# Hybrid four-mixer layer: the first attention pair is combined behind the third head's first branch, with one statistics buffer and shifted tiles

## The chip, the cores and the metric

The kernel runs on one core of a Trainium2 chip. The metric is the device time of one execution in microseconds (us). The core has TensorE (PE; its weight loads are listed as PEld), VectorE (DVE), ScalarE (ACT), GpSimd (POOL) and SyncE (SP), which here issues the transfers. Each runs its own queue of instructions in order and waits on semaphores. SBUF is the on-chip memory, PSUM holds the results of TensorE.

## The reference

One layer over 2048 tokens of width 1024: RMSNorm, one input projection to 13 slices of 256 columns, four mixers of which each is multiplied by the SiLU of a gate, one output projection, RMSNorm, residual. The change touches mixer A, a causal attention of four heads of 64. Each head is computed with three dilations (1, 4, 16) over blocks of 128, and the three results are weighted by their softmax denominators:

```python
for window, dil in DILATED_PAIRS:              # (128, 1), (512, 4), (2048, 16)
    o, lse = _dilated_branch(q, k, v, window, dil, slopes)
    outs.append(o); lses.append(lse)
w = jax.nn.softmax(jnp.stack(lses), axis=0)
o = jnp.einsum('gbhs,gbhsd->bhsd', w, jnp.stack(outs))
...
y = jnp.concatenate([ya * silu(ag), yb * silu(bg), yc * silu(cg), yd * silu(dg)], -1)
y = jnp.einsum('bse,ed->bsd', y, w_out)
return x + _rms_norm(y, post_g)
```

## The kernel before

All matrix products are made from fp32 values split in a high and a low part, with two or three matmuls for each product.

First stage (to about 690 us): in two halves of 1024 tokens the input is normalised and transposed (`hh`, `hl`), and projected. `proj_t` multiplies a weight tile of 128 columns (`w128`, three buffers) by 512 tokens into `ps_t`; `proj_m` has the tokens as weights and streams the 256 column tile (`w256`, one buffer, pool `pa`) into `ps_m`: 256 columns for each matmul. The mixers B, C and D are finished here. Queries, keys, values and the gate of mixer A go to DRAM (`qk_d`, `v_d`, `ag_d`), the finished parts to `yb_d`.

Attention stage (690 to about 925 us): `attention(p, tab)` does a pair of heads, p = 0 for the first and second, p = 1 for the third and fourth. For each head it loads `q2`, `k2a`, `k2b` and does the branches in the order dil 4, 16, 1. All these loads and the reordered `q2b` share seven buffers of 8 KiB (tag "m8"). `branch` computes scores (`ps_s`, L98), the exponentials (L652 on VectorE, L654 on ScalarE), transposes them (`ps_pt`, PSUM tag "t", three buffers), splits them (`pt_hi` L661, `pt_lo` L662), multiplies by the values (`ps_o`, two banks), and `finish` writes the result to `o01` or `o2` (L676, L677). For dil 4 and 16 `keep_stats` stores the statistics through DRAM (`std`, L742, L745); for dil 1 they are in `sv`, the others are read back (`sraw`, L603), and `weigh` (L751 to L768) makes the weights `wt`.

`combine` then takes a pair: three small transposes `ps_w` for each half of the tokens, sixteen products `ps_f` that spread the weights over a head's rows (also tag "t"), multiplications on VectorE (L789, L790), and for each 512 tokens two additions (L791, L792), the gate (`sga` loaded L796, multiplied L797) and the split into `ysa` (L809, L810; one buffer of 256 tokens), stored to `ya_d` (L811). For the first pair the elementwise part runs on GpSimd. `o2` and `wt` have one buffer each, `o01` is another tile in each pair.

Between them lie nine `partial(t)`: the output projection of 128 tokens over the mixers B, C and D (`ps_out`, stored to `part_d`, L849). They come last in the program, and `issue_after` holds each behind a chosen value product (`marks`).

In the last stage the second pair is combined and `final` finishes the tokens.

The order on each engine's queue is set when the program is built: a planner simulates the engines, and of the instructions it holds ready it takes the one that stands earlier in the program. On the chip the queues run in that fixed order. A tile that reuses a buffer waits until everything that used the earlier tile is done.

The names `align0` and `align1` are tiles that nothing uses; they shift those behind them.

Of the kernel before, what the change touches and what calls it, by code (L numbers as in the profile page):

```python
# [9 lines left out]
F32 = mybir.dt.float32  # L10
# [8 lines left out]
P = 128  # L19
SEQ = 2048  # L20
DM = 1024
KT = DM // P
GRP = 512
# [65 lines left out]
def hymba(ctx: ExitStack, tc: tile.TileContext, x, pre_g, w_in, sgu_g, sgu_w, sgu_b, pool_w,  # L89
          pool_scale, ret_g, w_out, post_g, cmix, catt, out, dbg=None, npart=9, spread=(0.3, 0.95)):  # L90
    nc = tc.nc
    V, A, G, T, D = nc.vector, nc.scalar, nc.gpsimd, nc.tensor, nc.sync
# [10 lines left out]
    cp = ctx.enter_context(tc.tile_pool(name="const", bufs=1))  # L103
# [15 lines left out]
    ya_d = [scratch(f"ya{g}", [P, 2, GRP]) for g in range(NG)]  # L119

    ident = cp.tile([P, P], F32, name="ident")
    cp.tile([P, 96], F32, name="align0")
    for _ in range(2):
        small.tile([P, 8], F32, tag="align1", name="align1")

# [22 lines left out]
    with ExitStack() as c1:  # L148
# [42 lines left out]
        W2 = 6  # L191
        hT = {}
        first = []

        def prologue(gs, step):

# [43 lines left out]
        def weights(col, n, eng=V, scales=(1.0,)):  # L240

            if n == P:
                w = p1.tile([P, 2, KT, n], F32R, tag="w128", bufs=3, name="w128")
            else:
                w = pa.tile([P, 2, KT, n], F32R, tag="w256", bufs=1, name="w256")
            kc = KT * P // n
            for k in range(0, KT, kc):
                raw = p1.tile([P, kc, n], F32, tag="raw", bufs=2, name="raw")
                D.dma_start(raw, w_src[:, k:k + kc, col:col + n])
                for i, sc in enumerate(scales):  # L250
                    cs = slice(i * n // len(scales), (i + 1) * n // len(scales))
                    hi, lo = w[:, 0, k:k + kc, cs], w[:, 1, k:k + kc, cs]
                    A.activation(hi, raw[:, :, cs], AF.Copy, scale=sc)  # L253
                    if sc == 1.0:
                        eng.tensor_tensor(lo, raw[:, :, cs], r32(hi), ALU.subtract)  # L255
                    else:
                        V.scalar_tensor_tensor(lo, raw[:, :, cs], sc, r32(hi), ALU.mult, ALU.subtract)
            return w
# [298 lines left out]

    marks = []

    def attention(p, tab):  # L560
        o01 = (big if p == 0 else po).tile([P, 2, SEQ], F32, tag="big" if p == 0 else "o01", name="att_o01")
        o2 = po.tile([P, SEQ], F32, tag="o2", name="att_o2")
        o = [o01[:, 0], o01[:, 1], o2]
        wt = pc.tile([P, 3, 2, 2, 2, 8], F32, tag="wt", bufs=1, name="wt")
        for s in range(2):
            h = 2 * p + s
            rows = slice(s * HD, (s + 1) * HD)
            other = slice((1 - s) * HD, (2 - s) * HD)
            q2 = pm.tile([P, SEQ], F32R, tag="m8", bufs=7, name="q2")
            k2a = pm.tile([P, SEQ], F32R, tag="m8", bufs=7, name="k2a")  # L570
            k2b = pm.tile([P, SEQ], F32R, tag="m8", bufs=7, name="k2b")
            D.dma_start(r32(q2[rows]), qk_d[0][p][rows, 0])
            D.dma_start(r32(q2[other]), qk_d[0][p][rows, 1])
            for z in (rows, other):
                D.dma_start(r32(k2a[z]), qk_d[1][p][rows, 0])
                D.dma_start(r32(k2b[z]), qk_d[1][p][rows, 1])
            for b, dil in enumerate(DILS):
                vt = pm.tile([P, 16, 2 * HD], F32R, tag="m8", bufs=7, name="att_v")
                dst = r32(vt)
                if dil == 1:  # L580
                    src = v_d[h].rearrange("(n t c) d -> c t n d", c=4, t=32)
                    for c in range(4):
                        D.dma_start(dst[c * 32:(c + 1) * 32], src[c])
                elif dil == 4:
                    D.dma_start(dst.rearrange("q (j c) d -> q j (c d)", j=4),
                                v_d[h].rearrange("(j q c) d -> q j (c d)", j=4, c=4))
                else:
                    D.dma_start(dst.rearrange("q r d -> q (r d)"), v_d[h].rearrange("(q r) d -> q (r d)", r=16))
                qb = q2
                if dil != 1:  # L590
                    qb = pm.tile([P, SEQ], F32R, tag="m8", bufs=7, name="q2b")
                    if dil == 4:
                        src = r32(q2).rearrange("p (j k c i) -> p c j k i", j=4, c=4, i=8)
                        dst = qb.rearrange("p (j c k i) -> p c j k i", j=4, c=4, i=8)
                        for c in range(4):
                            (V if c < 3 else G).tensor_copy(dst[:, c], src[:, c])
                    else:
                        V.tensor_copy(qb.rearrange("p (r w i) -> p r w i", r=16, i=8),
                                      r32(q2).rearrange("p (w r i) -> p r w i", r=16, i=8))
                if dil == 1:  # L600
                    sv = p2.tile([P, 3, 2, 16], F32, tag="sv", bufs=2, name="sv")
                    raw = p2.tile([64, P], F32, tag="sT", bufs=1, name="sraw")
                    D.dma_start(raw, st_d[h].rearrange("b z (n q) -> (b z n) q", q=P))  # L603
                    branch(h, dil, qb, k2a, k2b, vt, tab, o[b], sv[:, b])
                    weigh(sv, raw, wt[:, :, :, s])
                    continue
                st = p2.tile([P, 2, 16], F32, tag="stat", bufs=2, name="att_st")
                branch(h, dil, qb, k2a, k2b, vt, tab, o[b], st)
                keep_stats(h, b, dil, st)
        return o01, o2, wt  # L610

    def branch(h, dil, q2, k2a, k2b, vt, tab, o, st):
# [119 lines left out]
    def keep_stats(h, b, dil, st):  # L732

        pt = ps2.tile([P, GRP], F32, tag="t", bufs=N_T, name="ps_st")
        transpose(pt[:32, :P], st.rearrange("p z n -> p (z n)"))
        sT = p2.tile([32, P], F32, tag="sT", bufs=1, name="sT")
        V.tensor_copy(sT, pt[:32, :P])
        for z in range(2):
            dst, src = st_d[h][b, z], sT[z * 16:(z + 1) * 16]
            if dil == 4:  # L740
                for j in range(4):
                    D.dma_start(dst.rearrange("(j k c i) -> j c k i", j=4, k=16, c=4)[j],  # L742
                                src[j * 4:j * 4 + 4].rearrange("c (k i) -> c k i", i=8))
            else:
                D.dma_start(dst.rearrange("(w r i) -> r w i", r=16, i=8), src.rearrange("r (w i) -> r w i", i=8))  # L745
# [68 lines left out]
    def load_y(t, pool):  # L814
        raw = pool.tile([P, 6, P], F32, tag="yraw", bufs=2, name="yraw")
        D.dma_start(raw, yb_d[t // 4][:, t % 4])
        return raw

    def split_y(raw, pool, eng):

        ys = []
        for e in range(0, 6, 3):
            yt = pool.tile([P, 3, 2, P], F32R, tag="yt", bufs=2, name="yt")
            src = raw[:, e:e + 3]
            if eng is A:
                A.activation(yt[:, :, 0], src, AF.Copy)
            else:
                eng.tensor_copy(yt[:, :, 0], src)
            G.tensor_tensor(yt[:, :, 1], src, r32(yt[:, :, 0]), ALU.subtract)
            ys += [yt[:, j] for j in range(3)]  # L830
        return ys
# [12 lines left out]
    def partial(t):  # L844
        z = p3.tile([P, DM], F32, tag="z", bufs=2, name="z")
        ys = split_y(load_y(t, p3), p3, G)
        for n in range(2):
            A.activation(z[:, n * GRP:(n + 1) * GRP], out_proj(ys, range(2, 8), n, ps2, "part"), AF.Copy)
        D.dma_start(part_d[t * P:(t + 1) * P], z)  # L849
# [33 lines left out]
    with ExitStack() as c2:  # L883
        pm = c2.enter_context(tc.tile_pool(name="pm", bufs=1, reuse_waits="tile"))
        p2 = c2.enter_context(tc.tile_pool(name="p2", bufs=1, reuse_waits="tile"))
        ps2 = c2.enter_context(tc.tile_pool(name="ps2", bufs=2, space=PSUM, reuse_waits="tile"))
        tab = pm.tile([P, T_HEAD], F32, name="tab")
        D.dma_start(tab, catt)
        raw = p3.tile([P, DM], F32, tag="z", bufs=2, name="sel_raw")[:32]
        D.dma_start(raw, cmix[:32, C_SEL:])  # L890
        G.tensor_copy(sel, raw.rearrange("r (n m) -> r n m", m=P))
        o = attention(0, tab)
        for i in (1, 2, 3):
            out_weights(i, V if i == 2 else G)
        combine(0, o, ps2, "t", False, range(0, SEQ, GRP), G)
        o = attention(1, tab)
        for t in range(npart):
            with tc.issue_after(marks[int(len(marks) * (t + spread[0]) / npart * spread[1])]):
                partial(t)
        out_weights(0, G)  # L900
# [45 lines left out]
```

## Time and profile before

| what | value |
|---|---|
| median of 3 runs | 1059.02 us (1055.12 to 1059.49) |
| profiled execution | 1055.14 us, span 1053.4 us |
| granted TensorE clock, mean | 0.981 |
| ScalarE, VectorE, GpSimd busy | 376.4, 519.1, 228.0 us |
| DMA | 128.91 MB, mean 122 GB/s |

A row of the profile's groups gives line, engine, operation, the tiles read and written and the count, then busy time and the mean duration of one. A row of a timeline gives start and duration in us, and in brackets the idle time before it and what ended that. "L98" is the helper in which every matmul is recorded, "L101" that of the transposes.

### The profile page before, as it was taken

The numbers are of one execution on the slowest core, as the hardware profiler recorded it, in microseconds if no ns is written. First come the engines' busy times: TensorE is split into PE (matmuls) and PEld (weight loads), VectorE is DVE, ScalarE is ACT, GpSimd is POOL, SyncE is SP. The second block draws the span as 40 slices with busy tenths as digits, with TensorE's granted clock in tenths as the row PEclk, the third lists the DMA queues.
The fourth block names the chain that finished last, engine by engine and source line by source line (L and its number), as shares of the span: only waits on it lengthen the run. The fifth ranks groups of instructions, "written<-read, shape, count | busy, mean of one in ns | idle before, by whom it ended". The sixth has DMA issues, their size and how long they took to land.

```text
span 1053.4 us, 15825 instructions
## 1 busy us (share of the span) xinstructions
PE 1000.1 (95%) x5960; PEld 861.6 (82%) x5960; DVE 519.1 (49%) x1584; ACT 376.4 (36%) x871; POOL 228.0 (22%) x217
## 2 busy tenths in 40 slices
PE   5899999999999999999999999988999989899994
PEld 5889898998888998989898888777896979776773
DVE  7621215687323331031666222176876667727776
ACT  6320313132212431031221111297873878612231
POOL 2310002221133000002120124031116411313444
PEclk9999999999999999999999999996999989989998
DMA  7530222332423232040310661187474663445565
GB/s 284 146 100 21 81 80 81 121 107 72 123 68 103 91 95 65 1 140 34 128 61 21 154 179 41 62 219 203 102 212 141 161 202 77 154 142 181 175 250 220
DMA packets 110988, 128.91 MB, mean 122 GB/s; under 512 B 9888, under 2 KB 88992, under 8 KB 108864
## 3 DMA queue, kind: packets, MB, share of 16 engines
q1 hardware_dynamic: 110912, 127.90, 39.7%
q8 instruction: 47, 0.77, 0.3%
q14 instruction: 29, 0.24, 0.1%
HBM read 91.57 MB, written 36.31 MB: 121 GB/s over the span
## 4 chain that ended last, share of the span: by engine, by line
PE 82%; DMA 7%; DVE 6%; ACT 2%; issue 2%; POOL 1%; SPq 1%; DVEq 0%; POOLq 0%; ACTq 0%
PE ps_t L98 38%; PE ps_m L98 16%; PE ps_out L98 10%; PE ps_s L98 4%; PE ps_o L98 4%; PE ps_pt L101 3%; PE ps_of L98 2%; DMA out_dram<-z 2%; DMA k2b<-qk 2%; DMA cm<-in_cmix_dram 1%; PE ps_in L98 1%; POOL z L877 1%; PE ps_mix L98 1%; DMA raw<-in_w_in_dram 1%; PE ps_x L101 1%
## 5 line engine op out<-in xcount | busy, mean ns | idle before, releaser
L98 PE MATMUL ps_t<-hh,w 128*128 128x512 f32 x1152 | 366.9, 395 | 0.0
L98 PEld LDWEIGHTS ps_t<-hh,w 128*128 128x128 f32 x1152 | 215.9, 188 | 47.8 <-issue 3.4
L98 PE MATMUL ps_t<-hl,w 128*128 128x512 f32 x576 | 226.1, 393 | 0.0
L98 PE MATMUL ps_m<-w,hh 128*128 128x256 f32 x1024 | 190.1, 286 | 1.6 <-ACT hh L235 1.6
L98 PEld LDWEIGHTS ps_m<-w,hh 128*128 128x128 f32 x1024 | 161.3, 193 | 3.3 <-ACT hh L235 2.2
L98 PE MATMUL ps_out<-wo,yt 128*128 128x512 f32 x576 | 153.9, 406 | 0.6 <-DVE z L875 0.6
L98 PE MATMUL ps_m<-w,hl 128*128 128x256 f32 x512 | 147.7, 288 | 0.1
L98 PEld LDWEIGHTS ps_t<-hl,w 128*128 128x128 f32 x576 | 108.3, 188 | 23.2 <-issue 1.4
L98 PEld LDWEIGHTS ps_out<-wo,yt 128*128 128x128 f32 x576 | 105.6, 192 | 23.1 <-issue 2.8
L255 DVE TENSOR_TENSOR w<-raw,w 128x1024 fp32r<-128x1024 f32 x42 | 58.5, 1402 | 109.5 <-ACT w L253 109.5
L98 PEld LDWEIGHTS ps_m<-w,hl 128*128 128x128 f32 x512 | 98.8, 193 | 0.8 <-DVE hl L236 0.3
L253 ACT ACTIVATE w<-raw 128x1024 fp32r<-128x1024 f32 (+1 forms) x56 | 55.0, 997 | 67.7 <-PE ps_t L98 37.3
L652 DVE CUSTOM_DVE_ANT_0 att_p<-ps_s,tab 128x128 f32<-128x128 f32 (+1 forms) x192 | 60.6, 360 | 36.3 <-PE ps_s L98 29.6
L662 DVE TENSOR_TENSOR pt_lo<-ps_pt,pt_hi 128x512 fp32r<-128x512 f32 x80 | 51.5, 652 | 18.6 <-ACT pt_hi L661 18.2
L654 ACT ACTIVATE att_p<-att_p,att_st 128x128 f32<-128x128 f32 (+1 forms) x128 | 55.0, 433 | 6.9 <-DVE att_st L652 6.4
L98 PE MATMUL ps_o<-pt_hi,att_v 128*128 128x128 f32 (+1 forms) x204 | 53.9, 284 | 1.7 <-DVE att_o L677 1.7
L98 PE MATMUL ps_o<-pt_lo,att_v 128*128 128x128 f32 (+1 forms) x204 | 52.9, 294 | 0.4 <-DVE pt_lo L662 0.4
L101 PE MATMUL ps_pt<-ident,att_p 128*128 128x128 f32 x300 | 50.6, 285 | 2.7 <-ACT att_p L654 2.5
L449 POOL TENSOR_TENSOR d_g<-d_g,ret_b 128x512 f32<-128x512 f32 x8 | 10.4, 1296 | 184.6 <-ACT d_g L447 184.6
L661 ACT ACTIVATE pt_hi<-ps_pt 128x512 fp32r<-128x512 f32 x80 | 44.1, 565 | 12.0 <-PE ps_pt L101 6.4
L98 PEld LDWEIGHTS ps_o<-pt_hi,att_v 128*128 128x128 f32 x204 | 41.0, 201 | 4.3 <-DVE att_o L677 1.9
L877 POOL TENSOR_TENSOR z<-z,xr 128x1024 f32<-128x1024 f32 x15 | 35.8, 2390 | 32.4 <-DVE z L875 27.7
(174 smaller groups left out, 1409.9 us busy)
## 6 DMA issues: line engine op xcount, KB each, us to landing
raw<-in_w_in_dram SPq DMA_DIRECT2D x52, 512.0 KB
qk<-qk_s SPq DMA_DIRECT2D x16, 512.0 KB
att_v<-vd SPq DMA_DIRECT2D x8, 1024.0 KB
xr<-in_x_dram SPq DMA_DIRECT2D x16, 512.0 KB
out_dram<-z SPq DMA_DIRECT2D x15, 512.0 KB
xt<-in_x_dram SPq DMA_DIRECT2D x7, 1024.0 KB
yraw<-yb SPq DMA_DIRECT2D x16, 384.0 KB
partd<-z SPq DMA_DIRECT2D x9, 512.0 KB
```

The lines of the kernel that those rows point to most:

```text
L98: return T.matmul(o, lhsT, rhs, start=start, stop=stop, skip_group_check=True)
L101: T.transpose(o, i, ident[:n, :n])
L253: A.activation(hi, raw[:, :, cs], AF.Copy, scale=sc)
L255: eng.tensor_tensor(lo, raw[:, :, cs], r32(hi), ALU.subtract)
L449: G.tensor_tensor(o, o, ret_b.unsqueeze(1).broadcast_to([P, 2, 256]), ALU.mult)
L652: V.tensor_tensor_reduce(out=pr[:, u, :w], in0=ps[:, u, :w], in1=bb, scale=-SLOPES[h] * HD ** -0.5, scalar=3e38, op0=ALU.add, op1=ALU.min, ...
L654: A.activation(pr[:, u, :w], pr[:, u, :w], AF.Exp, bias=neg, scale=-1.0, accum_out=st[:, 1, n:n + 1])
L661: A.activation(hi, pt[:, :w], AF.Copy)
L662: V.tensor_tensor(lo, pt[:, :w], r32(hi), ALU.subtract)
L877: (V if last else G).tensor_tensor(z[:, ns], z[:, ns], xr[:, ns], ALU.add)
```

## The change

`combine` of the first pair no longer stands between the two calls of `attention`. It is passed as `between` to the second call and stands behind the third head's dil 4 branch and its `keep_stats`. For that `o2` and `wt` of a pair are asked for only at its first dil 1 branch. `sv`, which had two buffers in `p2`, is one tile of the constant pool, in the place of the 384 bytes of `align0`. In `pa` an unused tile of 448 bytes stands ahead of `w256` and one of 64 bytes behind it, and one of 480 bytes in `p3` behind the tiles of `partial`.

```diff
-    cp.tile([P, 96], F32, name="align0")
+    svs = cp.tile([P, 3, 2, 16], F32, name="sv")
...
+        align = []
...
             else:
+                if not align:
+                    align.append(pa.tile([P, 112], F32, name="align2"))
                 w = pa.tile([P, 2, KT, n], F32R, tag="w256", bufs=1, name="w256")
+                if len(align) == 1:
+                    align.append(pa.tile([P, 16], F32, name="align3"))
...
-    def attention(p, tab):
+    def attention(p, tab, between=None):
         o01 = (big if p == 0 else po).tile([P, 2, SEQ], F32, tag="big" if p == 0 else "o01", name="att_o01")
-        o2 = po.tile([P, SEQ], F32, tag="o2", name="att_o2")
-        o = [o01[:, 0], o01[:, 1], o2]
-        wt = pc.tile([P, 3, 2, 2, 2, 8], F32, tag="wt", bufs=1, name="wt")
+        o = [o01[:, 0], o01[:, 1]]
...
                 if dil == 1:
-                    sv = p2.tile([P, 3, 2, 16], F32, tag="sv", bufs=2, name="sv")
+                    if s == 0:
+                        o2 = po.tile([P, SEQ], F32, tag="o2", name="att_o2")
+                        o.append(o2)
+                        wt = pc.tile([P, 3, 2, 2, 2, 8], F32, tag="wt", bufs=1, name="wt")
+                    sv = svs
...
                 keep_stats(h, b, dil, st)
+                if between and s == 0 and b == 0:
+                    between()
...
         ys = split_y(load_y(t, p3), p3, G)
+        if t == 0:
+            p3.tile([P, 120], F32, name="align4")
...
-        combine(0, o, ps2, "t", False, range(0, SEQ, GRP), G)
-        o = attention(1, tab)
+        o = attention(1, tab, lambda o=o: combine(0, o, ps2, "t", False, range(0, SEQ, GRP), G))
```

## The prediction

> **What bounds the kernel now.** I read the page first (engine shares, the chain that ended last), then the busy time by stretch, then the waits and the timelines around the moved step.
>
> ```profile
> PE 1000.1 (95%) x5960; PEld 861.6 (82%) x5960; DVE 519.1 (49%) x1584; ACT 376.4 (36%) x871; POOL 228.0 (22%) x217
> PE 82%; DMA 7%; DVE 6%; ACT 2%; issue 2%; POOL 1%; SPq 1%; DVEq 0%; POOLq 0%; ACTq 0%
> 50.00:350.00 300.00, 299.84 (x1779) 257.57 (x1778) 119.28 (x320) 70.27 (x98) 51.93 (x59) 1.00 0.27 86
> 385.00:690.00 305.00, 303.11 (x1794) 260.08 (x1793) 100.80 (x282) 61.90 (x98) 46.34 (x47) 1.00 0.29 85
> 787.00:847.00 60.00, 58.46 (x359) 49.13 (x359) 40.01 (x153) 37.95 (x123) 28.97 (x35) 1.00 0.55 148
> 847.00:855.00 8.00, 3.56 (x26) 2.99 (x25) 4.13 (x10) 3.38 (x11) 2.75 (x4) 0.81 0.83 218
> 855.00:860.00 5.00, 5.00 (x23) 4.47 (x23) 3.72 (x12) 4.45 (x13) 1.06 (x2) 0.62 0.98 390
> 787.00:856.00 69.00, 63.02 (x387) 53.12 (x387) 44.15 (x164) 42.27 (x136) 32.16 (x39) 0.97 0.59 160
> 856.00:912.00 56.00, 56.00 (x384) 51.16 (x384) 42.11 (x151) 45.59 (x139) 7.84 (x11) 0.97 0.35 107
> 912.00:927.00 15.00, 10.85 (x46) 8.38 (x45) 8.42 (x16) 6.10 (x12) 6.21 (x5) 0.78 0.86 294
> ```
>
> The columns of a stretch are its length, then PE, PEld, DVE, ACT and POOL busy, the granted clock, the DMA share and GB/s. TensorE is full in the projections (299.84 of 300 us), so nothing can be gained there except by faster matmuls. In the attention stage the moved step's stretch, 787 to 847, is also full (58.46 of 60): the output projections of `partial` are there to fill TensorE when attention cannot go on. Behind it comes a hole, 847 to 855, in which 8.00 - 3.56 = 4.44 us are idle, followed by a stretch at a clock of 0.62. From 856 to 912 TensorE is full again, and at 912 there is a second hole.
>
> The waits of TensorE from 787 to 860 name what ended each idle time (total, times, longest):
>
> ```profile
> PE ps_s L98 <- DMA k2b<-qk: 4.1, 1, 4.1
> PE ps_w L101 <- DVE wt L768: 1.2, 1, 1.2
> PE ps_o L98 <- DVE att_o L677: 0.3, 1, 0.3
> PE ps_pt L101 <- DVE att_o L790: 0.3, 1, 0.3
> ```
>
> So the combine of the first pair costs TensorE directly only 1.2 us (its first transpose waits for the weights) and 0.3 us (an attention transpose waits for a PSUM buffer that the combine held). The large wait, 4.1 us, is the fourth head's first score waiting for its `k2b`.
>
> **What the moved step does now.** Its timeline on TensorE, the queue of SyncE, ScalarE and GpSimd:
>
> ```profile
> 794.24 0.38 PE L101 MATMUL ps_w<-ident,wt 128*32 128x128 f32 x2 [1.21 <-DVE wt L768]
> 798.14 0.79 PE L98 MATMUL ps_f<-wr,sel 32*128 32x384 f32 x3
> 801.44 4.47 PE L98 MATMUL ps_out<-wo,yt 128*128 128x512 f32 x18
> 811.22 0.97 PE L98 MATMUL ps_f<-wr,sel 32*128 32x384 f32 x3
> 812.46 1.05 PE L101 MATMUL ps_pt<-ident,att_p 128*128 128x128 f32 x7 [0.27 <-DVE att_o L790]
> 806.45 0.41 ACT L809 ACTIVATE ysa<-att_o 128x256 fp32r<-128x256 f32 x1
> 855.06 0.42 ACT L809 ACTIVATE ysa<-att_o 128x256 fp32r<-128x256 f32 x1 [4.63 <-DMA ya<-ysa]
> 855.56 0.73 POOL L810 TENSOR_TENSOR ysa<-att_o,ysa 128x256 fp32r<-128x256 f32 x1 [5.73 <-ACT ysa L809]
> 856.48 0.59 ACT L676 ACTIVATE att_o<-ps_o 64x512 f32<-64x512 f32 x1
> 841.28 0.56 SPq L811 DMA_DIRECT2D ya<-ysa  x1
> 841.94 1.08 SPq L745 DMA_DIRECT2D std<-sT  x2
> 846.58 0.46 SPq L603 DMA_DIRECT2D sraw<-std  x1
> 847.13 1.19 SPq L576 DMA_DIRECT2D k2b<-qk  x2
> 847.73 6.90 DMA k2b<-qk
> ACT ysa L809 <- DMA ya<-ysa: 12.5, 5, 4.6
> SPq L811 <- POOL ysa L810: 15.3, 6, 5.9
> ya<-ysa SPq DMA_DIRECT2D x8, 256.0 KB
> ```
>
> Three things are to be seen. First, from 798 to 812 the sixteen `ps_f` products pass before any attention transpose: both use PSUM tag "t" with three buffers, and the combine stands ahead in the program. Second, the combine has a long tail: eight `ysa` copies through one buffer, each waiting for the store of the one before, from 806.45 to 855.06. The pair's `o2` has one buffer too, so the third head's dil 1 branch cannot write its first result before the last `ysa` is read: that result is the L676 at 856.48, right behind the L810 at 855.56. Third, SyncE's queue runs in order: it held a `ya` store (waiting for GpSimd, up to 5.9 us), then statistics, then `sraw`, and only then the `k2b` that TensorE waited for.
>
> **The change, part by part.**
>
> The moved combine keeps all its instructions: 6 `ps_w` and 16 `ps_f` on TensorE, 2 `wr` and 8 `ysa` on ScalarE, 32 multiplications on VectorE, 24 on GpSimd, 8 `sga` loads and 8 `ya` stores on SyncE's queue. No engine gets work or loses it; only order changes. It moves behind the third head's dil 4 branch: 8 statistics stores and an `att_v` load on SyncE's queue, one quarter of `q2b` on GpSimd's, and the branch's transposes and splits.
>
> What that does to the branch is bounded by the other heads. First score and first statistics store of the third and the fourth head:
>
> ```profile
> 782.76 0.31 PE L98 MATMUL ps_s<-k2a,q2b 128*128 128x128 f32 x1
> 828.33 0.27 SPq L742 DMA_DIRECT2D std<-sT  x1
> 854.77 0.77 PE ps_s L98 x2
> 879.35 2.81 SPq L742 DMA_DIRECT2D std<-sT  x8
> ```
>
> The third head's dil 4 branch takes 828.33 - 782.76 = 45.6 us, the fourth's, which has no combine in it, 24.6 us. So the branch can end near 782.76 + 24.6 = 807.4, and dil 16, the release of its buffers and the fourth head's `k2b` can come up to 21 us earlier. By itself this is worth nothing, for TensorE was full. It is worth what it does to the hole.
>
> Removed: the 1.2 us (the queue then has scores and transposes of dil 4 there) and the 0.3 us: 1.5 us. If that cover is absent because dil 4 waits as well, the 1.5 us stay.
>
> Removed, as I take it: the hole. With `k2b` up to 21 us earlier, and `partial` fillers that were spent at 787 to 812 kept for later, there is work for its 4.44 us. The clock goes with it: 855 to 860 at 0.62 means (1.00 - 0.62) / 0.5 x 5 = 3.8 us at half rate, in which 1.9 us are lost (the half-rate time before 855 is idle already). Together 6.3 us, bounds 0 and 6.3. On that the Trainium skill, page "TensorE: Matmul & The Clock Gate", section "The HAM clock gate (the "warmup" mystery)", says the array falls to half clock after an idle window of about 3.4 us and needs as long busy to come back. The trace agrees: the 1.2 us wait left 787 to 847 at 1.00, the 4.1 us wait did not. By that rule a hole cut to 2 us would already give the 1.9 us back; the sum by it is the same when the hole closes.
>
> Added: the combine yields to dil 4, and its tail may end later. Every us beyond 856 delays the third head's dil 1 results, then the fourth head's banks; TensorE is full behind it, so it is paid in full once the fillers are used up. Bounds: nothing, even a gain, if the first `ps_f` still goes near 798 and ScalarE's 12.5 us of waits shrink; at most 807.4 - 798.14 = 9.3 us if it waits for the whole branch. I take 2 us, near the low end: from the second copy on the tail goes by store landings (12.5 us of waits), not by when the products come, and only the first chunk's delay counts.
>
> One statistics buffer: a wait of dil 1's first statistic for the head before's `weigh`. The last reader of that buffer, and the next head's first write:
>
> ```profile
> 790.56 0.21 DVE L759 TENSOR_TENSOR df<-ew,sv 128x48 f32<-128x48 f32 x1
> 827.68 0.08 DVE L652 DVE_READ_ACCUMULATOR2_ANT sv<- 128x1 f32 x1
> ```
>
> 37 us apart, two branches between them; even 21 us earlier it costs nothing. If it were tight, `q`'s scores would wait in VectorE's queue. `o2` and `wt` are only asked for later, at the branch that writes them; no cost, as `o2`'s release was the limit before too. The statistics tile takes the 384 bytes of the pad it replaces.
>
> The weight tile's 448 bytes, and the 64 and 480 byte pads: no instruction. They could change only how fast operands are read. The chain has runs of both kinds of projection:
>
> ```profile
> 94.03 23.03 PE ps_m L98 x192
> 117.06 10.91 PE ps_t L98 x48
> L98 PE MATMUL ps_m<-w,hh 128*128 128x256 f32 x1024 | 190.1, 286 | 1.6 <-ACT hh L235 1.6
> L98 PE MATMUL ps_m<-w,hl 128*128 128x256 f32 x512 | 147.7, 288 | 0.1
> ```
>
> `ps_m` reads the moved tile: 23.03 / 192 = 120 ns for 256 columns. `ps_t` reads other tiles at other places: 10.91 / 48 = 227 ns for 512. The second 256 columns cost 227 - 120 = 107 ns, so both kinds have the same 13 ns beside their columns. So the place shows no cost, and I take 0; the bounds are this 13 ns over the 1024 + 512 matmuls, 20 us either way.
>
> Sum: -1.5 - 6.3 + 2.0 + 0 = -5.8 us. The profiled execution took 1055.14 us (span 1053.4), so 1049.3 by its own time. The median of the runs, 1059.02, lies 3.9 us above it, so I put the median at 1053.
>
> **The rivals.**
>
> The hole only changes its place. SyncE's queue still carries 16 transfers of the combine between the fourth head's loads, and its order is planned ahead; a score is planned right behind a load that lands later than planned. For it: `k2b` was on its way until 847.73 + 6.90 = 854.6, and the queue waited 15.3 us for GpSimd. Against it: `k2b` is then free much earlier. Only the 1.5 us go, less the 2 us: 1058 to 1060.
>
> Slower: the tail of the combine becomes the bound. Place: the L676 behind the last `ysa`. For it: 855.56 and 856.48 touch already. From 7.8 us of delay on all is lost; at 9.3 us for the products and one more wait of 5.9 us on SyncE's queue it is 15.2 - 7.8 = 7.4 us slower: 1066. The Trainium skill, page "DMA: Bandwidth & Descriptors", section "Issuing engines are not separate DMA queues", says that all transfers run on the same 16 engines and interleave. The trace agrees: the 4.63 us wait for a 256 KB store has the `k2b` loads of 847.13 beside it. By that rule earlier loads fall under more of the tail and lengthen it, which is this rival.
>
> Faster by more: the attention's lead also fills the hole at 912 (15.00 - 10.85 = 4.15 us idle, and a clock of 0.78), because fillers are left over. Against it: fillers are freed at fixed marks, and 856 to 912 is full. It gives 1053 - 4 = 1049, and 1045 if the tail costs nothing and the clock stays up as well (2 us each). The weight tile's 20 us would lead to 1035 or less; nothing speaks for them.
>
> **How the numbers follow.** Forecast 0.47 (1049 to 1057, two thirds of it below the 0.5% line), hole in another place 0.24, slower 0.17, faster by more 0.12. Half a per cent, 5.3 us, is about what a measurement of this kernel can tell from no change; the line is 1053.7. Faster: two thirds of 0.47 and the 0.12 and a little, 0.46; slower: 0.17 and what of the moved hole is larger, 0.19; within: 0.35. The range takes in "faster by more" down to its 1045, with 2 us for the scatter of the runs, and "slower" to just short of its 1066: 1043 to 1065.
>
> **What the profile after would show.** Attention transposes between the `ps_f` from 795 to 812; the third head's dil 4 statistics near 807 to 817; `k2b` of the fourth head issued before 840; TensorE busy over 67 of the 69 us behind 787 (63.02 before), at clock 1.00. The forecast is wrong if the last L809 comes after 864, if a wait of over 3 us stands at the fourth head's first score, or if 192 `ps_m` no longer take 23.0 us.

## The result and the profile after

| | before | changed |
|---|---|---|
| median | 1058.30 us (1055.12 to 1059.49, 4 runs) | 1043.22 us (1041.70 to 1044.22, 4 runs) |
| ratio, 95% interval | | 0.9858 [0.9834, 0.9882] |
| span of the profiled execution | 1053.4 us | 1042.3 us |
| granted TensorE clock, mean | 0.981 | 0.985 |

The changed kernel is 1.4% faster, about 15 us, where the prediction had 1053 us and a gain of 5.8 us. The time stands at the low end of the range. A second series gave 0.9837 [0.9809, 0.9864]. Ratios are those on record: they are taken from all runs of a series, each beside the kernel before in the same series, and are not the quotient of two medians.

The page of the changed kernel first, then its chain of waits with the runs of the projections, then its stretches. The columns of a stretch are as in the prediction.

```profile
PE 991.9 (95%) x5960; PEld 854.1 (82%) x5960; DVE 518.7 (50%) x1584; ACT 377.3 (36%) x871; POOL 229.6 (22%) x217
```

```profile
94.78 22.61 PE ps_m L98 x192
117.39 10.88 PE ps_t L98 x48
140.84 21.97 PE ps_m L98 x192
469.14 21.97 PE ps_m L98 x192
```

```profile
787.00:856.00 69.00, 65.47 (x386) 55.39 (x385) 43.42 (x167) 41.58 (x132) 30.71 (x37) 0.95 0.64 180
856.00:912.00 56.00, 54.61 (x377) 49.91 (x376) 37.76 (x132) 44.04 (x132) 11.63 (x13) 1.00 0.28 78
912.00:927.00 15.00, 13.79 (x64) 10.62 (x62) 7.62 (x17) 4.70 (x10) 5.87 (x5) 1.00 0.95 357
```

Two things are to be seen. TensorE does the same 5960 matmuls in 8.2 us less busy time, and that begins in the first stage, which the moved combine does not touch: the first run of 192 `ps_m` takes 22.61 us where it took 23.03. And TensorE does not get ahead where the prediction wanted it: in the first hole the wait for `k2b` is 2.13 us and not 4.11, yet 787 to 856 holds 386 matmuls where it held 387 (390, if the stretch is moved by the 3.7 us that this kernel's attention stage is ahead). The second hole, 912 to 927, has 64 instead of 46 (71 in the stretch moved likewise).

### The profile page after: what moved, and what is told of

Its sections match the earlier page's. It is cut to its first block, busy times and chain, and to the rows that moved or that the text cites. A ratio compares the mean times of both kernels' runs of the same rounds, so it can differ in the third digit from the quotient of the medians.

```text
span 1042.3 us, 15827 instructions
## 1 busy us (share of the span) xinstructions
PE 991.9 (95%) x5960; PEld 854.1 (82%) x5960; DVE 518.7 (50%) x1584; ACT 377.3 (36%) x871; POOL 229.6 (22%) x217
## 4 chain that ended last, share of the span: by engine, by line
PE 82%; DMA 7%; DVE 6%; ACT 1%; POOL 1%; issue 1%; SPq 1%; DVEq 0%; POOLq 0%; ACTq 0%
PE ps_t L98 38%; PE ps_m L98 15%; PE ps_out L98 11%; PE ps_s L98 4%; PE ps_o L98 4%; PE ps_pt L101 3%; PE ps_of L98 2%; DMA k2b<-qk 2%; DMA cm<-in_cmix_dram 1%; DMA out_dram<-z 1%; DMA z<-partd 1%; PE ps_in L98 1%; POOL z L888 1%; DMA raw<-in_w_in_dram 1%; DVE att_p L661 1%
## 5 line engine op out<-in xcount | busy, mean ns | idle before, releaser
L98 PE MATMUL ps_m<-w,hh 128*128 128x256 f32 x1024 | 184.4, 282 | 3.0 <-ACT hh L236 2.9
L98 PEld LDWEIGHTS ps_m<-w,hh 128*128 128x128 f32 x1024 | 157.5, 189 | 4.7 <-ACT hh L236 3.5
L98 PE MATMUL ps_out<-wo,yt 128*128 128x512 f32 x576 | 150.5, 401 | 1.0 <-DVE z L886 0.6
L98 PE MATMUL ps_o<-pt_hi,att_v 128*128 128x128 f32 (+1 forms) x204 | 51.4, 276 | 2.9 <-DVE att_o L686 2.9
L98 PE MATMUL ps_o<-pt_lo,att_v 128*128 128x128 f32 (+1 forms) x204 | 50.7, 286 | 0.2 <-DVE pt_lo L671 0.2
L838 POOL TENSOR_TENSOR yt<-yraw,yt 128x384 fp32r<-128x384 f32 x32 | 33.6, 1053 | 47.9 <-ACT yt L835 46.6
```

The lines of the kernel that those rows point to most:

```text
L98: return T.matmul(o, lhsT, rhs, start=start, stop=stop, skip_group_check=True)
```

## The experiments

**1. The parts alone.** Theory at the start: the weight tile's place makes the projections faster, the move does the rest. Rival: all comes from the move.

`e1_shift_only`, the kernel before with the two pads around `w256`:

```diff
+                if not align:
+                    align.append(pa.tile([P, 112], F32, name="align2"))
                 w = pa.tile([P, 2, KT, n], F32R, tag="w256", bufs=1, name="w256")
+                if len(align) == 1:
+                    align.append(pa.tile([P, 16], F32, name="align3"))
```

> The kernel before with only the 448 byte tile ahead of the 256 column weight tile and the 64 byte tile behind it; every engine's queue has the same order as before. Theory A (the place of the weight tile sets how fast the matmuls that stream it follow each other): the eight stretches of 192 ps_m take 113 to 118 ns a matmul as in the changed kernel, not 120; the first attention score comes at about 686 us, not 690; everything behind it is only shifted, so 1058.3 - 4 = 1054. Rival B (the shorter ps_m stretches come from the new order, the place does nothing): 120 ns, 1058. Rival C (the place is worth all of the 15 us): 1043.

`e2_move_only`, the changed kernel without its three pads:

```diff
-                if not align:
-                    align.append(pa.tile([P, 112], F32, name="align2"))
-                if len(align) == 1:
-                    align.append(pa.tile([P, 16], F32, name="align3"))
...
-            p3.tile([P, 120], F32, name="align4")
```

> The changed kernel without its three pads (448, 64 and 480 bytes): the combine is moved, one statistics buffer; the queues have the changed kernel's order. Theory A: ps_m at 120 ns, first score at 690 us; behind it the changed kernel's attention and final stages, about 7 us shorter than before: 1058.3 - 7 = 1051, perhaps 1048 as the medians differ by 15 and the profiled spans by 11. Rival B: 1043. Rival C: 1058.

Measured: the shift alone 1054.11 us, ratio 0.9951 [0.9923, 0.9979]; the move alone 1047.40 us, 0.9903 [0.9870, 0.9936]. Their product, 0.9854, is what the whole change gives (0.9858). So both parts are real, and they add. (For the shift alone the medians, 1054.11 and 1056.99 us of before in that series, lie only 2.9 us apart; the ratio from all runs stands for 5.2 us, and its interval for 2 to 8.)

The chain of the shift alone:

```profile
93.02 22.61 PE ps_m L98 x192
115.64 10.88 PE ps_t L98 x48
467.38 21.97 PE ps_m L98 x192
```

and that of the move alone, beside the last such run of the kernel before:

```profile
93.65 23.03 PE ps_m L98 x192
471.16 23.23 PE ps_m L98 x192
```

```profile
471.54 23.23 PE ps_m L98 x192
```

From the start of the first run of `ps_m` to the end of the last, the move alone takes 471.16 + 23.23 - 93.65 = 400.74 us, and the kernel before 471.54 + 23.23 - 94.03 = 400.74 us. The shift alone takes 467.38 + 21.97 - 93.02 = 396.33 us, and the changed kernel 469.14 + 21.97 - 94.78 = 396.33 us. So 4.41 us come with the two pads; the instructions in the queues of the shift alone stand in the same order as before. The pads also move the tiles behind them by 512 bytes in all. That this is not the cause is shown below by a kernel with the same 512 bytes and `w256` at another place, whose `ps_m` gain nothing. `ps_t`, whose operands keep their place within 512 bytes, keeps its pace (10.88 and 10.91 us for 48).

The profiled execution of the shift alone has a span of 1053.6 us at a granted clock of 0.975, no shorter than that of before (1053.4 at 0.981). As an estimate, with the clock at 0.50 while it is down (as it is in the kernel before from 853 to 857), this is (0.981 - 0.975) / 0.5 x 1053.6 = 12.6 us more at half clock; up to 6.3 us can be lost in them, enough to hide 4.4 us. The medians, 10 runs against 13, show the gain; one profile would not have.

**2. The other pad and the statistics buffer.** `e3_no_pad4` is the changed kernel without the 480 byte pad. `e4_two_sv` has two statistics buffers again. That pad had to go for the second buffer: with both, the attention stage does not fit into SBUF, so the single buffer is what makes room for the pad.

```diff
-            p3.tile([P, 120], F32, name="align4")
```

> The changed kernel without the 480 byte tile behind partial's tiles. Theory A: the pad only moves tiles on the far side of SBUF, none of which is streamed by ps_m: 1043, within 2 us. Rival D (the pad is part of the gain, through ps_out or ps_f that read there): 1045 to 1050, with a ps_out cadence above the changed kernel's 227 ns.

```diff
-    svs = cp.tile([P, 3, 2, 16], F32, name="sv")
+    cp.tile([P, 96], F32, name="align0")
...
-                    sv = svs
+                    sv = p2.tile([P, 3, 2, 16], F32, tag="sv", bufs=2, name="sv")
...
-            p3.tile([P, 120], F32, name="align4")
```

> The changed kernel with two statistics buffers as before (the 480 byte pad is left out to make room). Theory A: one buffer costs and gains nothing, as its readers are done long before the next writer: the time of the run without the 480 byte pad, within 2 us. Rival E (one buffer delays the dil 1 branch or the weights): this kernel is 2 us or more faster than that run.

Measured 1045.16 us, 0.9882 [0.9843, 0.9921], and 1043.51 us, 0.9878 [0.9837, 0.9919]. Both intervals hold the changed kernel's 0.9858, so neither the pad nor the buffer shows an effect beyond the 0.4% either way of these intervals. The first run, 1045.16 us, lies at the edge of the rival's times, but the slower `ps_out` that the rival needs is not there: 22 in a row near 927 take 5.22 us without the pad and 5.21 us with it.

**3. Where the move's 1% comes from.** The move alone and the kernel before have the same first stage to 0.01 us, so they can be laid on one another. The stretches of the move alone:

```profile
787.00:856.00 69.00, 67.09 (x408) 56.52 (x407) 46.89 (x174) 43.98 (x139) 31.36 (x38) 0.98 0.57 159
856.00:912.00 56.00, 53.12 (x361) 47.86 (x361) 37.25 (x140) 43.59 (x135) 9.67 (x12) 1.00 0.35 108
912.00:927.00 15.00, 13.93 (x71) 11.21 (x70) 9.14 (x20) 7.27 (x14) 8.74 (x6) 1.00 0.66 226
```

From 787 to 912 it issued 408 + 361 = 769 matmuls; before it was 387 + 384 = 771. What the first hole gave, the next 56 us lost again. From 912 to 927 it issued 71 instead of 46. By 927 it is thus 23 ahead, 21 of them output projections of 512 columns. At 227 ns for one (10.91 / 48) the 23 are 5.2 us; with the 0.38 us by which this execution began its first run of `ps_m` earlier that is 5.6 us, and the last matmul starts 5.65 us earlier:

```profile
1039.18 0.84 PE L98 MATMUL ps_out<-wo,ysa 128*128 128x512 f32 x3
```

```profile
1033.53 0.84 PE L98 MATMUL ps_out<-wo,ysa 128*128 128x512 f32 x3
```

(before, then the move alone). So the move's worth lies at the second hole. The timelines there, of the kernel before on VectorE, on GpSimd, and on TensorE:

```profile
916.16 2.20 DVE L759 TENSOR_TENSOR df<-ew,sv 128x48 f32<-128x48 f32 x1 [0.31 <-ACT ew L758]
918.39 0.89 DVE L760 TENSOR_TENSOR nm<-df 128x16 f32<-128x16 f32 x1
919.31 0.91 DVE L761 TENSOR_TENSOR nm<-nm,df 128x16 f32<-128x16 f32 x1
921.24 0.90 DVE L765 CAST eh<-ew 128x48 fp32r<-128x48 f32 x1
915.88 2.41 POOL L555 TENSOR_TENSOR wo<-wo_raw,wo 128x1024 fp32r<-128x1024 f32 x1 [9.30 <-ACT wo L554]
918.25 3.85 POOL L829 TENSOR_TENSOR yt<-yraw,yt 128x384 fp32r<-128x384 f32 x4
913.92 4.42 PE L98 MATMUL ps_out<-wo,yt 128*128 128x512 f32 x18
922.50 0.61 PE L101 MATMUL ps_w<-ident,wt 128*32 128x128 f32 x2 [4.15 <-DVE wt L768]
```

TensorE has 18 `ps_out` in its queue ahead of `ps_w` and then waits 4.15 us for the last weights, and `weigh` is slow: L759 takes 2.20 us, where it took 0.21 at 790.56. It ends at 916.16 + 2.20 = 918.36, and the GpSimd split beside it at 915.88 + 2.41 = 918.29. The four `yt` splits end at about 918.25 + 0.96 = 919.21, 920.17, 921.14 and 922.10; L760 ends at 919.28, L761 at 920.22, the cast L765 at 922.14. Each of these four VectorE operations ends within 0.1 us behind a GpSimd operation. The reciprocal between them (L762), with one SBUF input, takes 0.25 us and is not stretched. This is what the Trainium skill, page "SBUF — State Buffer", section "Who interferes with whom", says of an exclusive lock: a VectorE instruction with two SBUF inputs, or one in a 2-port mode (it names casts, if their operands meet the conditions), and a GpSimd instruction that reads SBUF keep each other out for the whole instruction. The trace agrees, with 2.20 us in place of 0.21.

In the move alone TensorE has 26 `ps_out` there, and waits 1.07 us:

```profile
918.25 6.33 PE L98 MATMUL ps_out<-wo,yt 128*128 128x512 f32 x26
925.65 0.50 PE L101 MATMUL ps_w<-ident,wt 128*32 128x128 f32 x3 [1.07 <-DVE wt L773]
922.22 2.32 DVE L766 TENSOR_TENSOR nm<-nm,df 128x16 f32<-128x16 f32 x1
922.11 2.40 POOL L556 TENSOR_TENSOR wo<-wo_raw,wo 128x1024 fp32r<-128x1024 f32 x1
```

The stretching is not gone: L766 (L761 of before) takes 2.32 us and ends at 924.54, GpSimd's split at 924.51. `ps_w` comes 3.15 us later than before. What closes the hole here is that eight more products stand ahead of `ps_w` in the queue.

If the second hole is all that the move is worth, the kernel before must gain as much without any move, once this hole is closed in another way. Taking the splits off GpSimd should do it. `f1_vector_splits`:

```diff
-    def split_y(raw, pool, eng):
+    def split_y(raw, pool, eng, lo=None):
...
-            G.tensor_tensor(yt[:, :, 1], src, r32(yt[:, :, 0]), ALU.subtract)
+            (lo or G).tensor_tensor(yt[:, :, 1], src, r32(yt[:, :, 0]), ALU.subtract)
...
-            ys, es = split_y(yb or load_y(t, p4), py, A) + ys, (2, 3, 4, 5, 6, 7, 0, 1)
+            ys, es = split_y(yb or load_y(t, p4), py, A, V if t < npart + 3 else G) + ys, (2, 3, 4, 5, 6, 7, 0, 1)
...
-        out_weights(0, G)
+        out_weights(0, V)
```

> The kernel before, with the low parts of the first output weights (out_weights(0)) and of the first three final tiles split on VectorE, not GpSimd. Theory H (the second hole of before, 912 to 927, stands because GpSimd's two-input splits run beside the weights of the fourth head and hold up VectorE's small operations, 0.9 to 2.2 us each where 0.2 are usual, and because the final products wait for the same splits): the chain from the last ps_sv to ps_w falls from 9.2 to about 5 us, the wait of 4.15 us at ps_w goes, the clock stays up there: 5 to 7 us faster than before, 1051. Rival M (the hole closes only when the combine is moved, as the lead of the fillers decides): the wait stays over 3 us and the time within 2 us of before.

Measured 1048.18 us, ratio 0.9905 [0.9870, 0.9940]: the gain of the move, without it (10 us by the ratio, where 5 to 7 were expected). Its stretches and its timeline on VectorE and TensorE:

```profile
787.00:856.00 69.00, 63.69 (x390) 54.01 (x389) 44.83 (x165) 43.31 (x137) 32.30 (x39) 0.98 0.59 164
912.00:927.00 15.00, 15.00 (x73) 12.18 (x72) 7.71 (x22) 6.99 (x12) 0.00 (x0) 1.00 0.60 200
916.69 0.20 DVE L759 TENSOR_TENSOR df<-ew,sv 128x48 f32<-128x48 f32 x1
919.61 0.18 DVE L765 CAST eh<-ew 128x48 fp32r<-128x48 f32 x1
919.92 0.34 DVE L768 TENSOR_TENSOR wt<-ew,eh 128x16 f32<-128x16 f32 x3
913.64 10.24 PE L98 MATMUL ps_out<-wo,yt 128*128 128x512 f32 x43
```

The first hole is as before, the second is gone. Two things changed with one edit: the weights are written from 919.92 on and not from 922.27, and 43 products stand ahead of `ps_w` in place of 18. The chain from `ps_sv` to the written weights fell from 9.4 us (913.21 to 922.61) to 7.3 (912.92 to 920.26), not to the 5 expected. With the early weights alone TensorE, out of work at 918.3, would have waited some 2 us still. So, as an estimate, the waits on VectorE are about half of the 4.15 us, and the products the other half; an edit that makes only one of the two was not run.

**4. The two remedies together.** `h1_shift_and_splits` has the pads of the first and the edit of the last experiment, without the move. `g1_after_splits` is the changed kernel with that edit, `a1_changed_again` the changed kernel, and `g2_two_half_ysa` has its stores in halves through two buffers, to shorten the combine's tail:

```diff
-            for z in range(0, GRP, 256):
+            for z in range(0, GRP, 128):
...
-                ys = p2.tile([P, 2, 256], F32R, tag="ysa", bufs=1, name="ysa")
+                ys = p2.tile([P, 2, 128], F32R, tag="ysa", bufs=2, name="ysa")
```

> The kernel before with the 448 and 64 byte pads and the splits on VectorE of the run before, the combine not moved. Theory X (the move is worth only the second hole, which the splits close as well): it is as fast as the changed kernel, 1043 to 1046 (1048.2 of the splits alone less 3 to 4 of the pads). Rival Y (the move also shortens the stretch 787 to 912): 2 us or more slower than the changed kernel run beside it.

> The changed kernel with the same splits on VectorE. Theory X: nothing is left of the second hole in the changed kernel (its wait at ps_w is 1.2 us), so within 2 us of it. Rival Y: both gains add, 1037 to 1040.

> The changed kernel with the last copies of the first pair in tiles of 128 tokens and two buffers, not 256 and one (the same memory, twice the instructions). Theory T (the prediction's: the tail of the combine holds the third head's o2 and so the stretch 847 to 912): the last copy comes 4 us or more earlier than 862.8 and the time falls by 2 us or more. Rival X: TensorE has other products in that stretch, and the time stays within 2 us of the changed kernel whatever the tail does.

> The changed kernel once more, on the chip of the other three, as what they are compared with: 1043, ratio 0.986.

| | median us | ratio to before |
|---|---|---|
| shift and splits, no move | 1038.32 | 0.9834 [0.9805, 0.9864] |
| changed, and splits | 1042.88 | 0.9872 [0.9845, 0.9899] |
| changed, half stores | 1046.62 | 0.9905 [0.9873, 0.9937] |
| changed, again | 1039.92 | 0.9837 [0.9809, 0.9864] |

Without the move, but with the second hole closed in the other way, the kernel is as fast as the changed one; the splits add nothing to the move (3 us apart, not the 2 expected, but the intervals overlap). The two are remedies for one hole. The first hole is open in the run without the move (its score waits 3.53 us for `k2b`, 4.11 before), so closing it shows no worth beside that. None of the other three beats the changed kernel by more than its interval. `h1_shift_and_splits` came out 5 us below the lower end of its forecast, `a1_changed_again` beside it 3 us below.

The half stores did not do what they were made for: the kernel is 6.7 us slower than the changed one beside it, with intervals that do not overlap, so both the theory and the rival of this run fail. The last copy to `ysa` starts at 861.2 us, in the changed kernel on that chip at 865.1; but there all of attention runs 3.8 us later (the first start of L768, `weigh`'s L759 of before, is 738.5 and 742.3), so the tail is no shorter. The run still tells something. The rows of L768, the stretches to 907 and to 922, and a wait (first the half stores, then the changed kernel):

```profile
L768 DVE TENSOR_TENSOR df<-ew,sv x4: 194/288/461, 738.5 to 909.9; 128x48 f32<-128x48 f32 x4
856.00:907.00 51.00, 51.00 (x358) 47.06 (x357) 38.66 (x133) 44.12 (x130) 8.35 (x11) 1.00 0.29 80
907.00:922.00 15.00, 12.37 (x53) 9.44 (x52) 7.09 (x14) 4.59 (x10) 8.70 (x6) 0.89 0.75 267
912.82 0.39 PE L101 MATMUL ps_w<-ident,wt 128*32 128x128 f32 x2 [2.05 <-DVE wt L777]
```

```profile
L768 DVE TENSOR_TENSOR df<-ew,sv x4: 202/294/591, 742.3 to 918.5; 128x48 f32<-128x48 f32 x4
856.00:907.00 51.00, 47.97 (x331) 43.63 (x329) 34.74 (x128) 39.35 (x122) 9.03 (x11) 1.00 0.35 105
907.00:922.00 15.00, 15.00 (x85) 12.77 (x83) 8.92 (x16) 9.67 (x20) 8.38 (x6) 1.00 0.47 155
```

With TensorE full to 907 the last head's L768 starts 918.5 - 909.9 - 3.8 = 4.8 us earlier, and then the hole is back: 2.05 us of waiting, 53 matmuls where there were 85. One `ps_out` stands directly ahead of `ps_w` here and 25 behind it; in the changed kernel 26 stand ahead. An attention that ended earlier did not make the kernel faster, as the queue had the products that would fill the hole behind it; whether they could have run earlier was not looked into.

**5. Why the place matters.** In the kernels so far `hh`, `hl` and `w128` lie at a multiple of 512 bytes. `w256` lies there before, and at 448 bytes past it after. Theory: the two operands of a matmul must not lie at the same place modulo 512. Then any other place of `w256` would do, and a shifted `w128` would speed up `ps_t`. Three kernels in the changed order, with `w256` and `w128` at (64, 448), (256, 64) and (480, 256) bytes past the multiple; the first's edit, the others by other sizes:

```diff
+                if not pads:
+                    pads.append(p1.tile([P, 112], F32, name="align5"))
...
+                if len(pads) == 1:
+                    pads.append(p1.tile([P, 16], F32, name="align6"))
...
-                    align.append(pa.tile([P, 112], F32, name="align2"))
+                    align.append(pa.tile([P, 16], F32, name="align2"))
...
-                    align.append(pa.tile([P, 16], F32, name="align3"))
+                    align.append(pa.tile([P, 112], F32, name="align3"))
```

> The changed kernel's order, with the 256 column weight tile at 64 bytes past a multiple of 512 (changed kernel: 448 past, before: 0; the token tiles hh and hl stand at 0) and the 128 column tiles at 448 past (before and changed: 0). Theory P (a matmul is slowed when the tile it streams and the weights loaded meanwhile stand at the same place modulo 512 bytes): ps_m falls from 120 to 113 to 118 ns, and ps_t too, from 227 to 220 to 225 ns, which over 1728 ps_t is 3 to 12 us: 1032 to 1041. Rival Q (only the 448 of the streamed tile does it): ps_m at 120, ps_t at 227, 1047.

> As the run with 64 and 448, with 256 bytes for the 256 column tile and 64 for the 128 column tiles. Theory P: both cadences below 120 and 227 ns again, 256 being the farthest place: at or below 113. Rival Q: 120 and 227.

> As the run with 64 and 448, with 480 bytes for the 256 column tile and 256 for the 128 column tiles. Theory P: ps_m between its values at 448 and at 0, 116 to 120 ns; ps_t below 227. Rival Q: ps_m at 113 to 118 near 448, ps_t at 227.

One execution of each: 1048.56, 1056.92 and 1048.34 us. The chain of the second of them, and the same rows of all kernels as a table:

```profile
95.71 23.03 PE ps_m L98 x192
118.74 11.20 PE ps_t L98 x48
142.78 23.21 PE ps_m L98 x192
```

| `w256` past 512 | first 192 `ps_m` | second 192 | `w128` past 512 | 48 `ps_t` |
|---|---|---|---|---|
| 0 | 23.03 us | 23.23 us | 0 | 10.91 us |
| 448 | 22.61 | 21.97 | 0 | 10.88 |
| 64 | 22.61 | 22.81 | 448 | 11.00 |
| 256 | 23.03 | 23.21 | 64 | 11.20 |
| 480 | 22.72 | 22.91 | 256 | 10.93 |

The theory falls: at 256 bytes the operands lie apart and nothing is gained, and `ps_t` becomes slower at 64, not faster. The rival, that only 448 does it, falls too: 64 and 480 give 118 ns in the first run. That the place decides is shown; why is open. It can also cost: at 64 the 1728 `ps_t` are 1728 / 48 x (11.20 - 10.91) = 10.4 us slower by these rows, and that kernel's one execution stands 8.6 us above the one with 480 and 256, which has the same order. One thing speaks against a rule by the address alone: at 448 the first run of 192 goes at 22.61 / 192 = 117.8 ns for each matmul and the second at 114.4, while at every other place the second is 0.2 us slower than the first, with the same SBUF tiles in both runs. And both come back to the digit in each kernel that has this place and `w128` at 0.

## Why the prediction was right or wrong

*The pads, 0 us: wrong, they gave 4.4 us up to 495 us by the chain.* The failed step is "both kinds have the same 13 ns beside their columns. So the place shows no cost". That two kinds of matmul share an overhead says nothing on what it is made of; both also had both operands at a multiple of 512 bytes, so their rows could not tell place from a fixed cost. The bound of 20 us either way, from the same rows, held: 4.41 us up to 495 us. "Nothing speaks for them" was true of the rows, yet an effect without a row was given no part in the chances.

*The hole at 847, -6.3 us: wrong.* The failed step is "dil 16, the release of its buffers and the fourth head's `k2b` can come up to 21 us earlier". What it rests on came true: in the move alone the third head's dil 4 statistics leave at 805.51, near the 807 to 817 announced and 23 us earlier than before (800.20 in the changed kernel, whose first stage is 4.4 us shorter). But dil 16 did not follow. Its first scores and first transposes, in the kernel before, and then in the move alone with SyncE's queue:

```profile
825.56 0.22 PE L98 MATMUL ps_s<-k2a,q 128*128 128x128 f32 x1
829.60 0.60 PE L101 MATMUL ps_pt<-ident,att_p 128*128 128x128 f32 x4
```

```profile
812.21 0.22 PE L98 MATMUL ps_s<-k2a,q 128*128 128x128 f32 x1
829.47 2.28 PE L98 MATMUL ps_f<-wr,sel 32*128 32x384 f32 x5
831.87 1.16 PE L101 MATMUL ps_pt<-ident,att_p 128*128 128x128 f32 x8
805.51 3.17 SPq L747 DMA_DIRECT2D std<-sT  x8
840.37 0.81 SPq L750 DMA_DIRECT2D std<-sT  x2
845.75 1.35 SPq L575 DMA_DIRECT2D k2b<-qk  x2
```

The scores of dil 16 are 13.4 us earlier, its transposes 2.3 us later: between them, from 814.16 to 831.75, pass the sixteen `ps_f`. They pass before the transposes of dil 16 now as they passed before those of dil 4 in the kernel before. The prediction had seen that order ("the combine stands ahead in the program") and did not look for it at the combine's new place. So the statistics of dil 16 leave 1.6 us earlier than before (840.37 and 841.94), and `k2b` is issued 1.4 us earlier (845.75 and 847.13), and at 841.25 in the changed kernel, not before 840.

The wait for `k2b` fell all the same, from 4.11 us to 0.52 in the move alone: the score comes 1.3 us earlier, and TensorE gets there 2.3 us later, with work that was kept. In the ten profiles with the move this wait is 0.29 to 2.13 us, in the four without it 3.53 to 4.11. From 787 to 856 the move alone has 67.09 us of work, as announced (over 67 of 69); the changed kernel has 65.47. But the gain did not last. The rows of the move alone are the wait, then a stretch behind the last five `ps_f` in which the clock fell, then two new waits behind 856, where TensorE had been full before (56.00 of 56 us):

```profile
853.49 0.30 PE L98 MATMUL ps_s<-k2b,q2b 128*128 128x128 f32 x1 [0.52 <-DMA k2b<-qk]
830.00:840.00 10.00, 9.51 (x53) 7.67 (x53) 7.35 (x27) 5.82 (x18) 8.59 (x9) 0.83 0.49 151
865.08 4.46 PE L98 MATMUL ps_out<-wo,yt 128*128 128x512 f32 x18 [1.45 <-ACT z L853]
871.40 0.36 PE L98 MATMUL ps_s<-k2a,q2b 128*128 128x128 f32 x1 [1.39 <-DVE q2b L597]
```

That is the first rival, the hole that changes its place, in more than one piece, though neither wait is for a load, as that rival had it. And "a hole cut to 2 us would already give the 1.9 us back" does not hold here: behind the wait of 2.13 us the changed kernel has a clock of 0.61 from 851 to 855, and the stretch of 830 to 840 above fell to 0.83 with half a us idle.

*The transpose waits, -1.5 us:* both are gone, as predicted; a first score waits 0.48 us for another reason. They are part of the 769 against 771 matmuls and are not seen in the time by themselves.

*The combine's tail, +2 us, at most 9.3: wrong in size, and the price too.* The last `ysa` went from 855.1 to 866.9 us in the move alone (L814 in its numbering; 862.8 in the changed kernel), 11.8 us later, over the bound: the last five `ps_f` came at 829.47 where the last three had come at 811.22, since attention stood between them, too. By the prediction's "paid in full" this would have cost what lies beyond 856. Such a cost isn't seen: neither of the two waits behind 856 names the tail, and the kernel is faster.

```profile
L814 ACT ACTIVATE ysa<-att_o x8: 406/418/421, 824.0 to 866.9; 128x256 fp32r<-128x256 f32 x8
```

*One statistics buffer, 0:* right within the intervals (0.9878 with two buffers, 0.9882 with one, both without the 480 byte pad).

*The hole at 912:* a rival for "faster by more", worth 4 us at a chance of 0.12. It is where the move's gain arose, 25 matmuls or 5.7 us from 912 to 927. Its reason, output projections left over for the hole, was near the truth (26 ahead of `ps_w`, 18 before). What the prediction did not ask is why `weigh` was late; the 2.20 us of an operation of 0.21 us stood in the trace of before.

So the sign came out right by luck: of the 5.8 us forecast 6.3 us were put at a place that gave nothing, and the 15 us come from two others, each about 0.5 and 1%: a tile's address, and a hole 65 us behind the one looked at. Some 2 us of the move's gain lie behind the last matmul (span 1053.4 - 1039.18 = 14.2 us, and 1045.5 - 1033.53 = 12.0 us); what made that end shorter was not looked into.

## What to carry to other kernels

Before a hole on the bounding engine is priced, follow what fills it to the next place where that engine is full: work pulled forward is only a gain if the last hole behind it shrinks too. A step that takes a shared buffer ahead of its neighbours does so at its new place as well, so look there for what it held up at the old one. When a small operation takes ten times its usual time, look at what the engine beside it does and whether both end together; moving the split to the other engine, which also put more products ahead of the wait, gave here what a reordering of a whole stage gave. And two paces of one kind of matmul with the same shape ask for a run with its operand at another address, which costs one unused tile.

## What was not expected of the hardware

The pace of a matmul of 256 columns depends on where the streamed tile lies: 120 and 121 ns in the two runs at 0 and at 256 bytes past a multiple of 512, 118 and 119 at 64 and 480, and 118 and 114 at 448. The pace of 512 columns went from 227 to 233 ns with the weight tile at 64 (11.20 / 48). The cause is open.

The granted clock fell without a long idle time: 0.83 from 830 to 840 in the move alone, with 0.49 us idle in these 10 us and 0.07 in the 5 us before. What set it off was not looked into.

Small VectorE operations were stretched to the end of a GpSimd operation, from 0.21 to 2.20 us, and from 0.18 to 0.90 us for a cast.
